# Softmax sums in an attention loop: adding the two key tiles of some pairs on GpSimd first

## The chip, the cores and the metric

The kernel runs on one core of a Trainium2 chip. TensorE (PE) does the matrix products, VectorE (DVE), ScalarE (ACT) and GpSimd (POOL) the elementwise work; SyncE (SP) and GpSimd issue the DMAs. The metric is the device time of one execution in microseconds (us).

## What is computed

Two layers of a mixer trunk over 2048 latent tokens and 256 context tokens, width 1024, in float32. The part that the change touches is the softmax attention of eight heads:

```
s = jnp.einsum('bqhd,bkhd->bhqk', qi, k).astype(jnp.float32) * sm_scale
p = jax.nn.softmax(s, axis=-1).astype(v.dtype)
return jnp.einsum('bhqk,bkhd->bqhd', p, v)
```

In both layers the 2048 latent queries attend to 2304 keys (latent and context). In the first layer alone the 256 context queries attend to the 256 context keys as well. Around it stand projections, a short and a long depthwise convolution, gates and an output projection.

## The kernel before

A layer runs four phases: token work, features with convolutions, attention, projection. The Python code unrolls everything; a planner that knows priorities (the order of the code, shifted where the code asks for it) and modelled durations then fixes the order of the instructions on each engine when the program is built. Each engine works through its own list in order.

Attention works in jobs of one head and 512 queries: 32 jobs a layer. A job goes through its 18 key tiles of 128 keys in nine pairs; in the first layer every fourth job has a tenth pair, for the context queries, half as wide. For a pair:

- TensorE makes the scores of either tile in three products (L1073 to L1075), as every float32 factor is split into a high and a low part.
- ScalarE takes the exponential twice, once at full precision into `p` (L1076) and once rounded into `ph` (L1077), for either tile.
- GpSimd subtracts: the residue `pl = p - ph`, both tiles in one instruction of 128x1024 (L1078).
- VectorE adds `p` of either tile into `acc`, a PSUM tile, for the softmax sum (L1085; the first tile of a job is copied, L1083): two instructions of 128x512.
- TensorE multiplies the values by `ph` (L1100) and `pl` (L1101) into `po`. These four products are put off in the code until the next pair's scores and residue are issued (`flush`).

`p` has four buffers, `ph` and `pl` three, the scores three PSUM banks, `acc` and `po` one each. At a job's end (`close`) ScalarE copies `acc` and `po` out, and TensorE and VectorE reduce the sums.

The softmax is shifted by the maximum of each query. The maxima are made ahead: for the next job, 20 products (L985) into two PSUM banks, each reduced by VectorE (L986, L989), then turned by TensorE (L994) and written by ScalarE as row 96 of `Q` (L995), so that the score product subtracts them. `ahead` spreads these steps over the pairs, three pairs early, at raised priority. A job's first score needs its turned maxima.

In the first layer a job also carries one column block of modulation weights: a split by ScalarE and GpSimd (L190, L191) and 16 short products (L216). GpSimd's queue issues the loads of the next head's K, Q and values (L961 to L967), four in four jobs.

Of the kernel before, what the change touches and what calls it, by code (L numbers as in the profile page):

```python
# [9 lines left out]
F32 = mybir.dt.float32  # L10
# [3 lines left out]
ALU = mybir.AluOpType  # L14
# [4 lines left out]
P = 128  # L19
# [65 lines left out]
def trunk(ctx: ExitStack, tc: tile.TileContext, ins, out):  # L85
    nc = tc.nc
    V, S, G, PE = nc.vector, nc.scalar, nc.gpsimd, nc.tensor

    def pool(stack, name, **kw):
        return stack.enter_context(tc.tile_pool(name=name, bufs=kw.pop("bufs", 1), **kw))  # L90
# [5 lines left out]
    def psum(tag, name):  # L96
        return ps.tile([P, 512], F32, tag=tag, name=name, bufs={"a": 3, "b": 2}.get(tag, 1))
# [841 lines left out]
    def attention(l, start):  # L939
        es = ExitStack()  # L940
        tp = pool(es, f"A{l}", reuse_waits="tile")
        vp = pool(es, f"Av{l}", reuse_waits="tile")
        op = pool(es, f"Ao{l}", reuse_waits="tile", side="right")
        hp = [pool(es, f"Aa{l}", reuse_waits="tile", side="right"), pool(es, f"Ab{l}", reuse_waits="tile")]
        mp = pool(es, f"Am{l}", reuse_waits="tile") if l < DEPTH - 1 else None
        last = l == DEPTH - 1
# [12 lines left out]
        def load(h):  # L959
            K = hp[h % 2].tile([97, NTT, 2, P], F32R, tag="K", name="K")  # L960
            G.dma_start(K[0:NOPE], kn_d[l][h])  # L961
            G.dma_start(K[NOPE:97], kr_d[l][h])
            Q = hp[h % 2].tile([97, NTT, 2, P], F32R, tag="Q", name="Q")
            nq_ = (SEQ if last else NT) // P
            G.dma_start(Q[0:QK, :nq_], q_d[l][h, :, :nq_])
            Vt = vp.tile([P, NTT, P], F32R, tag=f"V{h % 2}", name="Vt")
            G.dma_start(Vt, v_d[l][h])  # L967
            kv[h] = (K, Vt, Q)
# [39 lines left out]
        def ahead(idx, share):  # L1008

            while len(sums) <= idx + 1 and len(sums) <= len(jobs):  # L1010
                steps, ends = [], []
                for j in jobs[len(sums) - 1]:
                    a, finish, turn = prepare(*j)
                    steps += [[st] for st in a]
                    steps[-1].append(finish)
                    ends.append(turn)
                steps[-1] += ends
                queue.extend(steps)
                sums.append(sums[-1] + len(steps))
            if idx < len(jobs):  # L1020
                goal = sums[idx] + round(share * (sums[idx + 1] - sums[idx]))
                while sums[-1] - len(queue) < goal:
                    with tc.high_priority(offset=PO):
                        for st in queue.pop(0):
                            st()
# [7 lines left out]
        def split_mods():  # L1033
            for _ in range(min(len(mods), 2 if idx < MD else 1)):
                i, j = mods.pop(0)
                w = mp.tile([P, KD, P], F32, tag="wm", name="wm", bufs=2)
                hi, lo = (mp.tile([P, KD, P], F32R, tag="wm" + c, name="wm" + c, bufs=2) for c in "hl")
                ready.append((i, j, halves(i, j, [w], hi, lo, V if MV else None)))

        def use_mods():  # L1040
            while ready:
                i, j, parts = ready.pop(0)
                modulation(i, (j,), lambda _: parts, mp.tile([4, P], F32, tag="mrow", name="mrow", bufs=2))
# [4 lines left out]
        def flush():  # L1048
            for st in late:
                st()  # L1050
            late.clear()

        for idx, job in enumerate(jobs):
            h = job[0][0]
            if job[0][1] == (1024 if h else 512) and h + 1 < H:
                load(h + 1)
            pairs = [(j, it) for j in job for it in range(j[3], NTT, 2)]
            for pi, ((h, s, n, k0), kt0) in enumerate(pairs):
                if idx == len(jobs) - 1 and pi == len(pairs) - AE:
                    mark = tc.cur_priority  # L1060
                K, Vt, Q = kv[h]
                first, final = kt0 == k0, kt0 == NTT - 2
                if first:
                    po = psum("c", "po")
                    acc = psum("d", "acc")
                p = tp.tile([P, 2, 512], F32, tag="p", name="p", bufs=4)
                ph = tp.tile([P, 2, 512], F32R, tag="ph", name="ph", bufs=3)
                pl = tp.tile([P, 2, 512], F32R, tag="pl", name="pl", bufs=3)
                scs = []
                for z in range(2):  # L1070
                    kt, qt = kt0 + z, slice(s // P, (s + n) // P)
                    sc = psum("a", "sc")
                    PE.matmul(sc[:, :n], lhsT=K[0:97, kt, 0], rhs=Q[0:97, qt, 0], start=True, stop=False)  # L1073
                    PE.matmul(sc[:, :n], lhsT=K[0:QK, kt, 0], rhs=Q[0:QK, qt, 1], start=False, stop=False)  # L1074
                    PE.matmul(sc[:, :n], lhsT=K[0:QK, kt, 1], rhs=Q[0:QK, qt, 0], start=False, stop=True)  # L1075
                    S.activation(p[:, z, :n], sc[:, :n], AF.Exp, scale=scale)  # L1076
                    S.activation(ph[:, z, :n], sc[:, :n], AF.Exp, scale=scale)  # L1077
                G.tensor_tensor(pl[:, :, :n], p[:, :, :n], ph[:, :, :n].bitcast(F32), op=ALU.subtract)  # L1078
                flush()

                for z in range(2):
                    if first and z == 0:
                        V.tensor_copy(acc[:, :n], p[:, 0, :n])  # L1083
                    else:
                        V.tensor_tensor(acc[:, :n], acc[:, :n], p[:, z, :n], op=ALU.add)  # L1085
                for z in range(2):
                    at = pi + (z + 1) / 2 + LEAD
                    if at <= len(pairs):
                        ahead(idx + 1, at / len(pairs))
                    else:  # L1090
                        ahead(idx + 1, 1)
                        ahead(idx + 2, (at - len(pairs)) / len(pairs))
                if pi == len(pairs) // 2:
                    split_mods()
                if pi == len(pairs) - ME:
                    use_mods()

                def products(kt0=kt0, n=n, Vt=Vt, ph=ph, pl=pl, po=po, first=first, final=final):
                    for z in range(2):
                        PE.matmul(po[:, :n], lhsT=Vt[:, kt0 + z, :], rhs=ph[:, z, :n], start=first and z == 0, stop=False)  # L1100
                        PE.matmul(po[:, :n], lhsT=Vt[:, kt0 + z, :], rhs=pl[:, z, :n], start=False, stop=final and z == 1)  # L1101

                def close(h=h, s=s, n=n, po=po, acc=acc):
                    accs = op.tile([P, 512], F32, tag="o", name="accs", bufs=3)
                    S.activation(accs[:, :n], acc[:, :n], AF.Copy, scale=2.0)
                    o = op.tile([P, 512], F32, tag="o", name="o", bufs=3)
                    S.copy(o[:, :n], po[:, :n])
                    nc.sync.dma_start(o_d[l][h, :, s : s + n], o[:, :n])

                    nq = n // P  # L1110
                    px = psum("e", "psum_t")
                    for t in range(nq):
                        PE.transpose(out=px[:, t * P : (t + 1) * P], in_=accs[:, t * P : (t + 1) * P], identity=idn)
                    sm = tp.tile([P, 4], F32, tag="sm", name="sm", bufs=2)
                    V.tensor_reduce(sm[:, :nq], px[:, :n].rearrange("p (t k) -> p t k", k=P), axis=AX.X, op=ALU.add)
                    V.reciprocal(rinv[l][:, s // P : s // P + nq, h], sm[:, :nq])

                late.append(products)
                if final:
                    late.append(close)  # L1120
# [130 lines left out]
    for l in range(DEPTH):  # L1251
        for phase in (tokens, features, attention, project):
            if SEQP and f"{l}{phase.__name__[0]}" not in SEQP:
                continue
            mark = phase(l, since(mark))
# [54 lines left out]
```

## Time and profile before

| what | value |
|---|---|
| median of 3 runs | 3695.61 us (3680.32 to 3699.47) |
| the profiled execution's own time | 3695.0 us |
| its span, first to last instruction | 3693.2 us |
| mean granted TensorE clock, share of full speed | 0.978 |
| busy: TensorE, VectorE, ScalarE, GpSimd | 3529.8, 2888.8, 2166.7, 2341.6 us |
| attention, first layer: first and last start of L1078's instructions in it, about | 815 to 1740 us |
| attention, second layer: the same | 2611 to 3502 us |

Busy time is the time in which an engine has an instruction running. Matmuls are pipelined, so that a busy TensorE is not TensorE at its peak. A wait is put down to the instruction that ended last before it.

### The profile page before, as it was taken

What the parts mean: (1) busy time and instruction counts of PE and PEld (TensorE: products, weight loads), DVE (VectorE), ACT (ScalarE), POOL (GpSimd) and SP (SyncE); (2) the same over time, 40 slices, a digit from 0 to 9 for tenths busy, and PEclk for the clock granted to TensorE, in tenths of its full rate; (3) what the DMA queues carried; (4) which work ended last, traced back from release to release, by engine and by line L of the source; (5) the groups of instructions that cost most, each with busy time, mean ns of one, the idle gap of its engine ahead of it and who ended that gap; (6) DMA issues with size and microseconds to landing.
All of it is one profiled execution on the core that took longest, in us unless ns stands there. A gap on an engine that the chain in (4) does not pass through costs nothing. (4 is left out here: it accounts for less than half of the span.)

```text
span 3693.2 us, 52810 instructions
## 1 busy us (share of the span) xinstructions
PE 3529.8 (96%) x17532; PEld 2916.9 (79%) x17532; DVE 2888.8 (78%) x5472; ACT 2166.7 (59%) x4328; POOL 2341.6 (63%) x1497
## 2 busy tenths in 40 slices
PE   7899999999999999999999989999999999998999
PEld 5787888887888787877788878887777777776777
DVE  5986977877888888888437878769988888888832
ACT  4665343247778777877445663433677777776720
POOL 4664344348888888877435654444687887877721
PEclk8999999999999999999999999999999999999999
DMA  7567333433333213312776773435232202222163
GB/s 219 171 186 205 82 107 110 113 112 78 79 79 88 61 45 82 85 58 64 232 231 207 215 213 100 114 99 125 80 76 61 41 27 61 59 61 75 43 197 114
DMA packets 394386, 411.47 MB, mean 111 GB/s; under 512 B 19168, under 2 KB 332128, under 8 KB 388960
## 3 DMA queue, kind: packets, MB, share of 16 engines
q1 hardware_dynamic: 387712, 333.87, 31.2%
q0 software_dynamic: 6400, 74.22, 8.9%
q8 instruction: 138, 2.26, 0.3%
q14 instruction: 136, 1.11, 0.1%
HBM read 266.72 MB, written 141.59 MB: 111 GB/s over the span
## 5 line engine op out<-in xcount | busy, mean ns | idle before, releaser
L1078 POOL TENSOR_TENSOR pl<-p,ph 128x1024 fp32r<-128x1024 f32 (+1 forms) x584 | 1387.2, 2397 | 276.2 <-ACT ph L1077 110.4
L986 DVE TENSOR_REDUCE mx<-pmax 128x1 fp32r<-128x512 f32 (+1 forms) x1296 | 795.1, 628 | 122.0 <-PE pmax L985 113.6
L1076 ACT ACTIVATE p<-sc 128x512 f32<-128x512 f32 x1168 | 713.4, 612 | 240.5 <-PE sc L1075 232.7
L1085 DVE TENSOR_TENSOR acc<-acc,p 128x512 f32<-128x512 f32 x1096 | 756.7, 690 | 55.9 <-ACT p L1076 29.5
L1077 ACT ACTIVATE ph<-sc 128x512 fp32r<-128x512 f32 x1168 | 703.8, 612 | 20.1 <-PE po L1100 16.2
L194 PE MATMUL pf<-hhf,wh 128*128 128x256 f32 (+1 forms) x1584 | 549.3, 348 | 18.2 <-ACT tg L867 8.4
L196 PE MATMUL pf<-hhf,wl 128*128 128x512 f32 (+1 forms) x1584 | 546.4, 347 | 4.5 <-POOL wl L191 3.7
L195 PE MATMUL pf<-hlf,wh 128*128 128x256 f32 (+1 forms) x1584 | 547.2, 346 | 0.0
L985 PE MATMUL pmax<-K,Q 96*128 96x512 f32 (+1 forms) x1296 | 465.0, 386 | 34.8 <-DVE mx L986 26.8
L1073 PE MATMUL sc<-Q,K 97*128 97x512 f32 x1168 | 476.5, 408 | 11.7 <-ACT ph L1077 9.3
L1101 PE MATMUL po<-pl,Vt 128*128 128x512 f32 x1168 | 467.9, 401 | 2.1 <-POOL pl L1078 1.8
L1074 PE MATMUL sc<-Q,K 96*128 96x512 f32 x1168 | 465.2, 398 | 0.0
L1100 PE MATMUL po<-ph,Vt 128*128 128x512 f32 x1168 | 461.9, 396 | 1.1 <-DMA Vt<-v_d 0.8
L1075 PE MATMUL sc<-Q,K 96*128 96x512 f32 x1168 | 462.4, 396 | 0.0
L191 POOL TENSOR_TENSOR wl<-wraw,wh 128x1024 fp32r<-128x1024 f32 x104 | 253.8, 2441 | 292.8 <-ACT wh L190 279.4
L747 DVE SCALAR_TENSOR_TENSOR cacc<-z,hv,cacc 128x384 f32<-128x384 f32 (+5 forms) x780 | 403.0, 561 | 14.3 <-ACT cacc L742 11.2
L194 PEld LDWEIGHTS pf<-hhf,wh 128*128 128x128 f32 x1584 | 303.7, 192 | 57.2 <-ACT wh L190 9.1
L196 PEld LDWEIGHTS pf<-hhf,wl 128*128 128x128 f32 x1584 | 303.0, 192 | 44.3 <-POOL wl L191 7.2
L985 PEld LDWEIGHTS pmax<-K,Q 96*128 96x128 f32 x1296 | 245.3, 190 | 116.9 <-DVE mx L986 58.6
L195 PEld LDWEIGHTS pf<-hlf,wh 128*128 128x128 f32 x1584 | 303.8, 192 | 36.1
L1073 PEld LDWEIGHTS sc<-Q,K 97*128 97x128 f32 x1168 | 222.2, 190 | 71.3 <-ACT ph L1077 20.0
L1075 PEld LDWEIGHTS sc<-Q,K 96*128 96x128 f32 x1168 | 224.5, 192 | 51.5
(257 smaller groups left out, 6189.0 us busy)
## 6 DMA issues: line engine op xcount, KB each, us to landing
wraw<-in_w_in SPq DMA_DIRECT2D x108, 512.0 KB
q_d<-sg SPq DMA_DIRECT2D x68, 384.0 KB
wm<-in_w_mod SPq DMA_DIRECT2D x46, 512.0 KB
v_d<-vs SPq DMA_DIRECT2D x36, 512.0 KB
kn_d<-sg SPq DMA_DIRECT2D x72, 256.0 KB
K<-kn_d POOLq DMA_DIRECT2D x16, 1152.0 KB, 8.5
Vt<-v_d POOLq DMA_DIRECT2D x16, 1152.0 KB, 14.8
o_d<-o SPq DMA_DIRECT2D x64, 256.0 KB
```

The costliest lines, as they stand in the source:

```text
L194: PE.matmul(out_, lhsT=ahi, rhs=bhi, start=first, stop=False)
L195: PE.matmul(out_, lhsT=ahi, rhs=blo, start=False, stop=False)
L196: PE.matmul(out_, lhsT=alo, rhs=bhi, start=False, stop=last)
L985: PE.matmul(pm[:, :w], lhsT=Q[0:QK, s // P + t, 0], rhs=K[0:QK, a // P : (a + w) // P, 0], start=True, stop=True)
L986: V.tensor_reduce(part[:, t, c : c + 1], pm[:, :w], axis=AX.X, op=ALU.max)
L1073: PE.matmul(sc[:, :n], lhsT=K[0:97, kt, 0], rhs=Q[0:97, qt, 0], start=True, stop=False)
L1075: PE.matmul(sc[:, :n], lhsT=K[0:QK, kt, 1], rhs=Q[0:QK, qt, 0], start=False, stop=True)
L1076: S.activation(p[:, z, :n], sc[:, :n], AF.Exp, scale=scale)
L1077: S.activation(ph[:, z, :n], sc[:, :n], AF.Exp, scale=scale)
L1078: G.tensor_tensor(pl[:, :, :n], p[:, :, :n], ph[:, :, :n].bitcast(F32), op=ALU.subtract)
L1085: V.tensor_tensor(acc[:, :n], acc[:, :n], p[:, z, :n], op=ALU.add)
L1101: PE.matmul(po[:, :n], lhsT=Vt[:, kt0 + z, :], rhs=pl[:, z, :n], start=False, stop=final and z == 1)
```

## The change

For some pairs GpSimd adds the two tiles of `p` into a new tile `both` (two buffers) right behind the residue, and VectorE adds `both` to `acc` in one instruction. These are pairs 1, 4 and 7 of nine in the last layer, and pairs 1 and 4 in the first. The other pairs stay as they were. The sums are the same but for the order of the additions.

```diff
                 G.tensor_tensor(pl[:, :, :n], p[:, :, :n], ph[:, :, :n].bitcast(F32), op=ALU.subtract)
+                paired = pi % 3 == 1 and (last or pi < 6)
+                if paired:
+                    both = tp.tile([P, 512], F32, tag="both", name="both", bufs=2)
+                    G.tensor_tensor(both[:, :n], p[:, 0, :n], p[:, 1, :n], op=ALU.add)
                 flush()
 
-                for z in range(2):
-                    if first and z == 0:
-                        V.tensor_copy(acc[:, :n], p[:, 0, :n])
+                for x in [both[:, :n]] if paired else [p[:, z, :n] for z in range(2)]:
+                    if first:
+                        V.tensor_copy(acc[:, :n], x)
+                        first = False
                     else:
-                        V.tensor_tensor(acc[:, :n], acc[:, :n], p[:, z, :n], op=ALU.add)
+                        V.tensor_tensor(acc[:, :n], acc[:, :n], x, op=ALU.add)
+                first = kt0 == k0
```

## Rows read from the trace of the kernel before

**Rows 1.** The page: busy us, share of the span and instructions by engine.
```profile
PE 3529.8 (96%) x17532; PEld 2916.9 (79%) x17532; DVE 2888.8 (78%) x5472; ACT 2166.7 (59%) x4328; POOL 2341.6 (63%) x1497
```

**Rows 2.** Groups by form, layer 1, 2720 to 3263: busy, mean ns | idle before.
```profile
L1078 POOL TENSOR_TENSOR pl<-p,ph 128x1024 fp32r<-128x1024 f32 x180 | 428.4, 2402 | 104.3 <-PE pmax L985 58.6 <-issue 21.1 <-ACT ph L1077 16.8
L1085 DVE TENSOR_TENSOR acc<-acc,p 128x512 f32<-128x512 f32 x341 | 236.3, 693 | 25.9 <-ACT p L1076 18.4
```

**Rows 3.** Groups by form, layer 0, 936 to 1500.
```profile
L191 POOL TENSOR_TENSOR wml<-wm,wmh 128x1024 fp32r<-128x1024 f32 x20 | 47.9, 2393 | 26.6 <-ACT wmh L190 26.6
...
L1078 POOL TENSOR_TENSOR pl<-p,ph 128x512 fp32r<-128x512 f32 x5 | 6.5, 1298 | 0.1
```

**Rows 4.** Windows of attention: stretch, length; busy of PE, PEld, DVE, ACT, POOL; clock.
```profile
936.00:1500.00 564.00, 563.01 (x2786) 453.84 (x2784) 494.42 (x918) 444.42 (x836) 492.49 (x227) 1.00 0.29 72
...
2615.00:2720.00 105.00, 98.06 (x430) 77.79 (x431) 97.28 (x155) 76.37 (x147) 83.94 (x41) 0.98 0.22 53
2720.00:3263.00 543.00, 536.83 (x2362) 426.58 (x2361) 475.92 (x821) 410.22 (x781) 438.70 (x201) 1.00 0.23 52
3263.00:3505.00 242.00, 226.91 (x960) 176.55 (x959) 210.65 (x333) 175.69 (x345) 183.32 (x81) 0.96 0.25 65
```

**Rows 5.** Waits, layer 1, 2720 to 3263: us in total, times, longest.
```profile
PEld pmax L985 <- DVE mx L986: 19.3, 53, 0.6
...
PE pmax L985 <- DVE mx L986: 4.0, 16, 0.4
...
PEld po L1101 <- POOL pl L1078: 0.6, 2, 0.3
```

**Rows 6.** Waits, layer 0, 936 to 1500.
```profile
POOL wml L191 <- ACT wmh L190: 26.6, 10, 3.4
...
PEld pmax L985 <- DVE mx L986: 1.4, 5, 0.4
```

**Rows 7.** Waits, the opening of layer 1's attention, 2615 to 2720.
```profile
PE pmax L985 <- DVE mx L986: 6.5, 6, 2.7
```

**Rows 8.** Timeline, layer 0, one job: start, us, instruction, [idle before].
```profile
1069.54 0.48 PE L994 MATMUL pmt<-idr,mx 128*97 128x128 f32 x4
...
1075.61 0.22 PE L216 MATMUL pm<-wmh,s 128*4 128x128 f32 x1
...
1076.51 0.22 PE L216 MATMUL pm<-wml,s 128*4 128x128 f32 x1
...
1079.89 0.69 DVE L1083 COPY acc<-p 128x512 f32<-128x512 f32 x1 [0.73 <-ACT p L1076]
```

**Rows 9.** Timeline of TensorE, layer 1, the end of a job.
```profile
2989.72 0.40 PE L1073 MATMUL sc<-Q,K 97*128 97x512 f32 x1
2989.95 0.40 PE L1074 MATMUL sc<-Q,K 96*128 96x512 f32 x1
...
2994.17 0.50 PE L985 MATMUL pmax<-K,Q 96*128 96x512 f32 x1 [0.40 <-DVE mx L986]
2994.51 0.40 PE L1101 MATMUL po<-pl,Vt 128*128 128x512 f32 x1
...
2995.44 0.48 PE L994 MATMUL pmt<-idr,mx 128*97 128x128 f32 x4
...
2996.73 0.42 PE L1073 MATMUL sc<-Q,K 97*128 97x512 f32 x1
```

**Rows 10.** Timeline of GpSimd, layer 1, the same job.
```profile
2972.15 14.19 POOL L1078 TENSOR_TENSOR pl<-p,ph 128x1024 fp32r<-128x1024 f32 x6 [4.83 <-PE pmax L985]
2986.56 2.40 POOL L1078 TENSOR_TENSOR pl<-p,ph 128x1024 fp32r<-128x1024 f32 x1 [0.21 <-ACT ph L1077]
2989.14 2.41 POOL L1078 TENSOR_TENSOR pl<-p,ph 128x1024 fp32r<-128x1024 f32 x1 [0.17 <-ACT ph L1077]
2991.84 2.38 POOL L1078 TENSOR_TENSOR pl<-p,ph 128x1024 fp32r<-128x1024 f32 x1 [0.28 <-PE po L1100]
2999.85 2.41 POOL L1078 TENSOR_TENSOR pl<-p,ph 128x1024 fp32r<-128x1024 f32 x1 [5.63 <-PE pmax L985]
```

## The prediction, made before the result was known

> **What bounds the kernel now.** I read the page's busy shares first, then the windows of the two attention stages, then the waits inside them, and last the timeline at the seam between two jobs.
>
> TensorE is busy 96% of the span, VectorE 78%, GpSimd 63% [rows 1]. These are averages over stages; the change lives in attention alone, so the windows count. I chose one steady stretch of 20 jobs in each layer (180 residues at nine a job in [rows 2]; one split of modulation weights a job, x20, in [rows 3]). Layer 0: 564 us, so 28.2 us a job, TensorE 563.0 (99.8%), VectorE 494.4 (88%), GpSimd 492.5 (87%). Layer 1: 543 us, 27.15 us a job, TensorE 536.8 (98.9%), VectorE 475.9 (88%), GpSimd 438.7 (81%); the granted clock is 1.00, full speed, in both [rows 4]. So three engines stand close together and TensorE leads. A change that only empties VectorE can give back no more than what TensorE loses to VectorE.
>
> The waits say where that is. In layer 1's stretch the maximum products (L985) wait for VectorE's reductions (L986), which free their two PSUM banks: 19.3 us ahead of weight loads in 53 places and 4.0 us ahead of matmuls in 16 [rows 5]. In layer 0's stretch the same wait is 1.4 us [rows 6]. In the opening of layer 1's attention it is 6.5 us ahead of matmuls [rows 7].
>
> The timeline shows why the layers differ. In layer 0 the next job's shifts are turned (L994, at 1069.54) ten microseconds before that job's first add (1079.89) [rows 8]: the look-ahead maxima are done early. In layer 1 they are turned at 2995.44 and the next job's first score follows at 2996.73, just behind a maximum product that stood 0.40 us for VectorE [rows 9]. The maxima have fallen back to the last moment, because layer 1 has the shorter job with the same VectorE work. At that seam GpSimd stands idle too, 5.63 us between the last residue of one job and the first of the next; before it the residues run nearly back to back [rows 10].
>
> The Trainium skill (Perfetto Trace Analysis, Identifying the Most-Contended Engine) says matmul busy time is a poor measure of headroom and weight-load busy share a better one. The trace agrees: weight loads fill 453.8 of 564 us (80.5%) in layer 0 and 426.6 of 543 (78.6%) in layer 1 [rows 4], so the slack is layer 1's.
>
> **The change, part by part.** Paired are pairs 1 and 4 of nine in layer 0 (64 in its 32 jobs) and pairs 1, 4, 7 in layer 1 (96): 160.
>
> *Removed from VectorE:* one 128x512 add into PSUM for each, 0.693 us [rows 2]; 160 x 0.693 = 111 us, 2.08 us a job in layer 1, 1.39 in layer 0. In layer 0 nothing waits for it, so it is worth between 0 and 32/20 x 1.4 = 2 us; I take 0. In layer 1 it takes VectorE from 23.8 to 21.7 us a job, below layer 0's 24.7, in a job that is only 1 us shorter; the maxima should then run ahead as they do there. What that is worth has three measures. (a) TensorE's own idle time in the stretch, 543 - 536.8 = 6.2 us: 32/20 x 6.2 = 10 us over the layer. (b) Layer 0's pace: its stretch holds 424 matmuls more. 320 are modulation products at (1076.51 - 1075.61)/15 = 0.06 us [rows 8], 19 us; 50 belong to five context pairs, half of the 0.23 us spacing of a full one [rows 9], 6 us; the other 54, short ones, I estimate at 5 us. Without them layer 0 would take 534 us for what costs layer 1 543: 9 us, or 14 over 32 jobs. (c) All waits on the reductions, 23.3 us: 37 us over 32 jobs. The ends are 10 and 37; weight-load waits partly hide under a running matmul, but a matmul that starts late also hides inside the busy count, so I take the middle, 23.5 us. In the opening I take half of the 6.5 us, 3.2. The close of the layer, 3263 to 3505, loses 15.1 us of TensorE [rows 4], but VectorE splits output weights there too; I take nothing for it.
>
> *Added to GpSimd:* one 128x512 add each. The residue in that shape takes 1.298 us [rows 3], so 2.6 us a job in layer 0 and 3.9 in layer 1, 208 us in all. The bounds: nothing where GpSimd would have been idle, the whole 208 us where it is full. Layer 0: 24.6 + 2.6 = 27.2 of 28.2 us. Layer 1: 21.9 + 3.9 = 25.8 of 27.15. Both fit; what covers them is the idle time at the seam and between residues, so I take 0 in the steady stretches. If that cover were gone, the next residue would be late, then the product that reads it (L1101), and TensorE stops, as it works in order. At the end of the last job nothing covers them: the adds of pairs 4 and 7 delay the last residues, 2.6 us.
>
> The Trainium skill (GPSIMD Engine Reference, Engine selection) says elementwise adds belong on VectorE, since GpSimd is about twice as slow with two inputs. The trace agrees, 1.298 against 0.693 us; by that rule the change trades 111 us for 208 and should lose wherever GpSimd is full, which is the last rival below.
>
> *Moved and waiting:* VectorE's add for a paired pair now waits for GpSimd, a residue (2.40 us [rows 2]) and an add behind the exponentials. Queued behind it on VectorE are reductions, and the maximum products wait for these. If the planner puts the add too early, each costs up to 1.3 us of VectorE, 3.9 us a job in layer 1, against the 2.08 us saved; but VectorE idles 12%, and the order is made with the dependency known: 0 taken, and the upper end is another way into the second case. ScalarE reuses a p buffer only after GpSimd's add, one of four buffers, so 0. The loads of a head's keys, queries and values sit in GpSimd's queue (four issues for four jobs); they move by an add or two and are issued about a job before their first use: 0. Matmul counts, DMAs and exponentials do not change.
>
> **Sum.** -23.5 - 3.2 + 2.6 = -24.1 us, on the profiled execution's own 3695.0 us: 3671 us. The median shown is 3695.6, so the reference is the same. 0.5% is 18.5 us, about what runs spread over 19 us can tell from no change.
>
> **The rivals.**
> *Forecast, 0.50:* layer 1's maxima catch up. 3671 us, own range 3655 to 3688. For it: the wait is almost wholly in layer 1, and VectorE loses exactly there the most. Against it: the planner's order, not only the durations, sets the seam.
>
> *Nothing measurable, 0.26:* 3688 us. TensorE's floor is closer than I think (measure (a), 10 us), and some of it is paid back in waits for residues. For it: TensorE is 98.9% busy already [rows 4].
>
> *GpSimd becomes the bound, 0.24:* slower, about 3718. Place: the last residues of a job. In layer 1 three adds push the ninth residue by 3 x 1.3 less the 0.66 us of gaps among the last residues, 3.2 us; it ended at 2991.84 + 2.38 = 2994.22 and its product started at 2994.51 [rows 9, 10], so 0.3 us is slack and up to 2.9 us a job, 93 us, could reach TensorE. In layer 0 GpSimd also stands 26.6 us in 20 jobs behind the modulation weights' ScalarE copy [rows 6] with 2.39 us residues of weights behind it [rows 3]: 27.2 + 1.3 = 28.5 against 28.2, 0.3 us a job, 10 us. It decides from the point where the seam's 5.63 us no longer takes up the lateness; I price it at 10 us in layer 0 and a seventh of the 93, 13, in layer 1, with the forecast's gain gone: 3695 + 23 = 3718. It reaches from 3705, layer 0 alone, to 3798, all of it. Against it: today TensorE waits 0.6 us for residues in 543 [rows 5], and the seam's idle time is larger than the adds.
>
> **How the numbers follow.** The forecast case lies beyond -0.5% in four of five of its outcomes: 0.40, and 0.10 within. The second case is within, save 0.02 faster and 0.01 slower. The third is slower in 0.20 and within in 0.04. Faster 0.42, same 0.37, slower 0.21. The range runs from 3652, which is measure (c) with the opening and layer 0's 2 us (3695 - 37 - 3 - 2 = 3653), to 3714, just short of the third case's middle; some 0.06 is left out below and 0.13 above.
>
> **What would show it.** Right: layer 1's jobs at about 26.4 us, the wait of maximum products for reductions down from 23.3 us in 20 jobs to under 8, the turn of the shifts several microseconds ahead of the next job's scores, GpSimd at 93 to 97% in both layers, and 160 adds of about 1.3 us. Wrong: weight loads or matmuls of L1101 waiting for residues by more than 10 us a stretch, layer 0's job longer than 28.3 us, or VectorE's adds waiting for GpSimd with reductions queued behind them. A longer stall at the change of stages, where VectorE's and ScalarE's orders are made anew, would make the time wrong without touching the argument.

## The result, and the profile after

The change made the kernel slower: 3731.6 us median (3727.5 to 3733.8, six runs) against 3693.1 us, ratio 1.0103, 95% interval 1.0084 to 1.0123. Forecast was 3671, with 3652 to 3714 as the range: the kernel got slower where it was to get faster, and the time lies outside. The profiled execution took 3733.8 us, its span is 3732.0 against 3693.2. In the changed kernel the lines behind L1078 have moved: GpSimd's add is L1082, VectorE's adds are L1090 (L1085 before), the products L1106 and L1107 (L1100, L1101), the copies that close a job L1111 and L1113.

The page's busy line and the windows of the 20 steady jobs in either layer (columns as in [rows 4]):

```profile
PE 3547.5 (95%) x17532; PEld 2910.1 (78%) x17532; DVE 2796.5 (75%) x5312; ACT 2207.2 (59%) x4328; POOL 2534.9 (68%) x1657
```
```profile
943.00:1524.00 581.00, 572.42 (x2779) 452.82 (x2778) 473.55 (x874) 454.43 (x836) 540.99 (x267) 1.00 0.28 70
...
2752.00:3298.00 546.00, 541.79 (x2381) 423.97 (x2380) 449.73 (x780) 427.63 (x781) 512.31 (x261) 1.00 0.22 52
```

Against [rows 1] VectorE lost 92 us and GpSimd gained 193. GpSimd is busy 93% (541.0 of 581) and 94% (512.3 of 546), where [rows 4] has 87% and 81%. Layer 0's 20 jobs now need about 580 us in place of 564. Groups by form in layer 1, 2752 to 3298:

```profile
L1078 POOL TENSOR_TENSOR pl<-p,ph 128x1024 fp32r<-128x1024 f32 x180 | 429.4, 2401 | 33.6 <-ACT ph L1077 23.0 <-DVE mx L986 6.3 <-DVE acc L1090 1.5
...
L1107 PE MATMUL po<-pl,Vt 128*128 128x512 f32 x362 | 143.7, 397 | 0.0
...
L1082 POOL TENSOR_TENSOR both<-p 128x512 f32<-128x512 f32 x60 | 77.4, 1290 | 0.0
```

The add takes 1.29 us, as estimated, and GpSimd's idle time ahead of residues fell from 104.3 [rows 2] to 33.6 us. TensorE never waits for a residue (0.0 ahead of L1107). The waits of the same stretch, and then those of layer 0, 943 to 1524:

```profile
PEld sc L1073 <- ACT ph L1077: 26.2, 80, 0.6
...
ACT ph L1077 <- PE po L1106: 8.1, 30, 0.6
...
PEld pmax L985 <- DVE mx L986: 4.5, 12, 1.0
...
PE sc L1073 <- ACT ph L1077: 1.8, 11, 0.2
...
PE pmax L985 <- DVE mx L986: 0.9, 3, 0.6
```
```profile
ACT ph L1077 <- PE po L1106: 30.5, 55, 3.8
...
PEld pmax L985 <- DVE mx L986: 14.8, 29, 3.8
PEld sc L1073 <- ACT ph L1077: 12.1, 34, 0.6
PE pmax L985 <- DVE mx L986: 6.0, 8, 3.4
```

In layer 1 the wait of maximum products for reductions did fall, from 19.3 + 4.0 [rows 5] to 4.5 + 0.9 us. In its place the score products wait 28 us for ScalarE: a score bank comes free when `ph` is written, and `ph` is written when a product has read the buffer it reuses. In layer 0 there is no gain to set against this: the wait for reductions rose from 1.4 us [rows 6] to 20.8.

Where the 39 us lie is read from the starts of the ScalarE copies of `po` that close the jobs. Two of them, at the ends of heads 0 and 6 in layer 1:

```profile
2762.26 0.59 ACT L1113 COPY o<-po 128x512 f32<-128x512 f32 x1
...
3415.18 0.65 ACT L1113 COPY o<-po 128x512 f32<-128x512 f32 x1
```

(3415.18 - 2762.26) / 24 jobs = 27.21 us a job. "First head", also called the opening, is the time from the layer's first score to the copy that ends head 0. The last column counts the matmuls that start in the stage.

| stage, us | before | after | difference | matmuls |
|---|---|---|---|---|
| layer 0, first head | 130.4 | 140.6 | +10.2 | 623, 643 |
| layer 0, 24 steady jobs | 28.20 each | 28.95 each | +18.0 | 3332, 3331 |
| layer 0, last head | 133.3 | 124.0 | -9.3 | 546, 519 |
| between the attentions | 845.9 | 841.0 | -4.9 | 4281, 4289 |
| layer 1, first head | 129.3 | 147.4 | +18.1 | 533, 567 |
| layer 1, 24 steady jobs | 27.06 each | 27.21 each | +3.6 | 2818, 2839 |
| layer 1, last head | 133.0 | 135.8 | +2.8 | 493, 458 |
| all else | | | +0.3 | 4906, 4886 |

The stages do not hold the same work: the new order makes products for later jobs earlier, in the openings, and the last heads have fewer left. At the 0.23 us spacing of [rows 9] an estimate for the same work is +6, +18 and -3 us in layer 0, and +10, -1 and +11 in layer 1 (first head, steady jobs, last head).

So three places carry the loss: layer 0's jobs, the openings and the last head of layer 1. In that last head TensorE is idle 19.3 us in place of 12.3, and its matmuls wait for ScalarE ahead of their scores (3.1 us before); the waits from 3415 to 3551:

```profile
PE sc L1073 <- ACT ph L1077: 12.1, 20, 2.2
```

The opening of layer 1 can be followed in the timeline. First GpSimd in the changed kernel, then VectorE, then TensorE:

```profile
2636.23 2.38 POOL L1078 TENSOR_TENSOR pl<-p,ph 128x1024 fp32r<-128x1024 f32 x1
2638.59 1.28 POOL L1082 TENSOR_TENSOR both<-p 128x512 f32<-128x512 f32 x1
2639.84 4.65 POOL L1078 TENSOR_TENSOR pl<-p,ph 128x1024 fp32r<-128x1024 f32 x2
...
2638.02 6.62 DVE L164 TENSOR_SCALAR csq<-cva 128x264 int32<-128x264 int32 x1
2644.56 0.68 DVE L986 TENSOR_REDUCE mx<-pmax 128x1 fp32r<-128x512 f32 x1
...
2645.30 1.33 PE L985 MATMUL pmax<-K,Q 96*128 96x512 f32 x2 [4.72 <-DVE mx L986]
...
2703.72 1.20 PE L985 MATMUL pmax<-K,Q 96*128 96x512 f32 x2 [4.46 <-DMA Q<-q_d]
```

L164 is a shift of integer words from SBUF to SBUF, part of a reciprocal root that the stage still owes. Its record lasts from 2638.02 to 2644.64, and GpSimd's unbroken row of four instructions ends at 2644.49. The reduction behind it on VectorE is late, TensorE stands 4.72 us for it, and 58 us on it stands another 4.46 us for a load of Q. The same row in the kernel before, with GpSimd beside it:

```profile
2621.99 2.53 DVE L164 TENSOR_SCALAR csq<-cva 128x264 int32<-128x264 int32 x1
...
2621.97 2.40 POOL L1078 TENSOR_TENSOR pl<-p,ph 128x1024 fp32r<-128x1024 f32 x1 [0.58 <-POOL pl L1078]
2624.85 2.40 POOL L1078 TENSOR_TENSOR pl<-p,ph 128x1024 fp32r<-128x1024 f32 x1 [0.48 <-ACT ph L1077]
```

There a gap of 0.48 us came after one residue, at 2624.37, and L164 ended at 2624.52. But the long hold adds little to the sum. Waits of the whole opening, after (2615 to 2762) and then before (2599 to 2728):

```profile
PE pmax L985 <- DVE mx L986: 8.5, 7, 4.7
...
PE pmax L985 <- DMA Q<-q_d: 4.5, 1, 4.5
```
```profile
PE pmax L985 <- DVE mx L986: 7.0, 8, 2.7
```

Before, more of VectorE's instructions were held, each for a shorter time. Nor did the load of Q, which is that of the next head, come late. The first is its issue after, the second the first product that reads it before:

```profile
2684.34 0.52 POOL L965 DMA_DIRECT2D Q<-q_d  x1
```
```profile
2694.00 0.63 PE L985 MATMUL pmax<-K,Q 96*128 96x512 f32 x2
```

The load was issued 69.5 us behind the layer's first score, 68.8 before (at 2667.67), and landed 19.2 us on, 19.1 before. Its first reader is the layer's 81st product of L985, as the first head's four jobs have 20 each. That reader was next in TensorE's order 84.4 us behind the first score, where before it came at 95.2. The order had drawn the look-ahead forward; the load stayed where it was.

The last part is TensorE's granted clock. The windows of the whole opening, after and then before (the clock is the third last figure), each with the stretches in it at 0.50, which is 1.2 GHz:

```profile
2615.00:2762.00 147.00, 132.47 (x567) 103.52 (x566) 118.36 (x195) 96.03 (x178) 114.98 (x65) 0.93 0.28 68
...
2642.50:2649.33 6.83, 4.03 (x9) 3.10 (x10) 6.76 (x12) 0.60 (x1) 1.98 (x1) 0.50 0.00 0
2659.57:2666.40 6.83, 5.97 (x14) 4.72 (x15) 5.53 (x11) 3.62 (x7) 2.37 (x1) 0.50 0.00 0
2700.53:2707.36 6.83, 3.64 (x11) 3.01 (x12) 1.56 (x3) 1.50 (x3) 0.78 (x2) 0.50 0.14 31
```
```profile
2599.00:2728.00 129.00, 120.77 (x533) 94.74 (x533) 115.10 (x187) 88.56 (x170) 95.40 (x50) 0.99 0.30 74
...
2643.68:2647.09 3.41, 3.41 (x10) 2.64 (x9) 3.41 (x7) 2.73 (x7) 1.78 (x1) 0.50 0.00 0
```

The first and the third of these begin within the stops of 4.72 and 4.46 us. TensorE is busy 13.6 us at the lower clock in place of 3.4; half of that is lost against full speed, an estimated 6.8 us in place of 1.7. In all TensorE stands idle 14.5 us in place of 8.2 and is busy 11.7 us longer. By estimate 5 of the 11.7 us are the clock, and the rest, about 7, goes to the 34 matmuls more (8 us at 0.23). Of the 6.3 us more of idle time 4.5 are the wait for Q and 1.5 the reductions.

### The profile page after: what moved, and what is told of

The parts are those of the page before. It is cut to its first block, busy times and chain, and to the rows that moved or that the text cites. A ratio compares the mean times of both kernels' runs of the same rounds, so it can differ in the third digit from the quotient of the medians.

```text
span 3732.0 us, 52967 instructions
## 1 busy us (share of the span) xinstructions
PE 3547.5 (95%) x17532; PEld 2910.1 (78%) x17532; DVE 2796.5 (75%) x5312; ACT 2207.2 (59%) x4328; POOL 2534.9 (68%) x1657
## 5 line engine op out<-in xcount | busy, mean ns | idle before, releaser
L1078 POOL TENSOR_TENSOR pl<-p,ph 128x1024 fp32r<-128x1024 f32 (+1 forms) x584 | 1386.4, 2390 | 157.2 <-ACT ph L1077 105.8
L1076 ACT ACTIVATE p<-sc 128x512 f32<-128x512 f32 x1168 | 692.9, 599 | 298.8 <-PE sc L1075 277.3
L1077 ACT ACTIVATE ph<-sc 128x512 fp32r<-128x512 f32 x1168 | 644.4, 596 | 92.6 <-PE po L1106 83.9
L194 PE MATMUL pf<-hhf,wh 128*128 128x256 f32 (+1 forms) x1584 | 549.4, 348 | 19.1 <-ACT tg L867 8.3
L1090 DVE TENSOR_TENSOR acc<-acc,p 128x512 f32<-128x512 f32 (+1 forms) x776 | 535.8, 691 | 29.0 <-ACT p L1076 2.4
L1073 PE MATMUL sc<-Q,K 97*128 97x512 f32 x1168 | 490.6, 420 | 21.6 <-ACT ph L1077 19.1
L985 PE MATMUL pmax<-K,Q 96*128 96x512 f32 (+1 forms) x1296 | 448.4, 387 | 44.7 <-DVE mx L986 33.7
L1107 PE MATMUL po<-pl,Vt 128*128 128x512 f32 x1168 | 467.3, 400 | 0.0
L1106 PE MATMUL po<-ph,Vt 128*128 128x512 f32 x1168 | 463.1, 397 | 0.7 <-DMA Vt<-v_d 0.7
L985 PEld LDWEIGHTS pmax<-K,Q 96*128 96x128 f32 x1296 | 245.7, 191 | 119.2 <-DVE mx L986 58.1
```

Source lines behind the costliest of these rows:

```text
L194: PE.matmul(out_, lhsT=ahi, rhs=bhi, start=first, stop=False)
L985: PE.matmul(pm[:, :w], lhsT=Q[0:QK, s // P + t, 0], rhs=K[0:QK, a // P : (a + w) // P, 0], start=True, stop=True)
```

## The experiments

Each ratio is to the runs of the kernel before beside it, with its 95% interval; "layer 1: first head, steady job" are the stages of the table above. The table has all of them; the diffs below are against the changed kernel unless said.

| run | us | ratio | layer 0: first head, steady job | layer 1: first head, steady job |
|---|---|---|---|---|
| the change | 3731.6 | 1.0103 (1.0084-1.0123) | 140.6, 28.95 | 147.4, 27.21 |
| layer 1 alone | 3722.6 | 1.0073 (1.0054-1.0092) | 130.4, 28.19 | 147.2, 27.21 |
| layer 0 alone | 3700.6 | 1.0010 (0.9997-1.0022) | 140.6, 28.98 | 130.0, 27.00 |
| relief only | 3691.6 | 0.9989 (0.9976-1.0003) | 132.1, 28.29 | 127.7, 26.96 |
| load only | 3725.9 | 1.0074 (1.0056-1.0092) | 140.1, 28.74 | 150.3, 27.28 |
| products first | 3729.0 | 1.0089 (1.0068-1.0111) | 142.8, 28.65 | 148.1, 27.21 |
| four `ph`, `pl` | 3724.0 | 1.0077 (1.0055-1.0099) | 144.7, 28.56 | 143.8, 27.12 |
| narrow add | 3676.9 | 0.9960 (0.9942-0.9979) | 134.2, 28.76 | 130.9, 26.64 |
| add later | 3731.9 | 1.0096 (1.0074-1.0118) | 140.7, 28.99 | 147.0, 27.21 |
| planned with a fast GpSimd | 3835.8 | 1.0375 (1.0354-1.0396) | 134.9, 29.38 | 138.0, 30.72 |
| its control | 3737.6 | 1.0106 (1.0089-1.0124) | 130.4, 28.87 | 128.1, 28.07 |
| one pair, layer 1 | 3689.9 | 0.9979 (0.9967-0.9991) | 131.3, 28.18 | 127.9, 27.05 |
| two pairs, layer 1 | 3694.1 | 1.0001 (0.9989-1.0013) | 130.7, 28.21 | 142.6, 26.48 |
| two, not first head | 3688.7 | 0.9979 (0.9965-0.9992) | 131.4, 28.19 | 129.2, 26.75 |
| change, not first heads | 3699.4 | 1.0003 (0.9990-1.0017) | 130.1, 28.81 | 129.1, 27.25 |
| one pair, layer 0 | 3678.9 | 0.9944 (0.9925-0.9963) | 138.0, 27.96 | 129.1, 27.07 |
| two pairs and weights moved, layer 0 | 3719.5 | 1.0061 (1.0041-1.0080) | 143.3, 29.12 | 130.5, 27.00 |
| weights moved alone | 3724.7 | 1.0080 (1.0055-1.0105) | 134.3, 28.95 | 129.0, 27.07 |
| one pair, then two, not first heads | 3674.8 | 0.9941 (0.9919-0.9964) | 130.3, 28.10 | 129.1, 26.77 |

The jobs of a layer that a run leaves alone repeat within 0.1 us, but its last head and the stages behind do not: layer 1's last head is 127.0 us where layer 0 alone was changed, 133.0 before, with 493 matmuls in both. Differences of under about 10 us in a total are therefore not read as effects of an edit.

**Either layer alone.**

```diff
-paired = pi % 3 == 1 and (last or pi < 6)
+paired = last and pi % 3 == 1
```

> Pairs 1, 4, 7 of the last layer alone; the first layer as before. The trace of the changed kernel puts some 20 us of its 38 into the first layer's attention and some 20 into the last layer's (opening and close above all). If the loss is a cost of the loaded stretch itself, this kernel loses the last layer's half: 3710 to 3716. If the loss of the last layer came from what the first layer did to the order, about 3693.

```diff
+paired = not last and pi % 3 == 1 and pi < 6
```

> Pairs 1 and 4 of the first layer alone. Cost of the loaded stretch: first layer's jobs at 29.0 us as in the changed kernel, 3710 to 3716 in all, and the last layer's jobs back at 27.15 us.

The two layers are independent: each layer's attention is as in the full change (147.2 and 27.21; 140.6 and 28.98). Layer 1 alone costs 0.7%; layer 0 alone costs 19 us inside its attention, but the total shows 0.1%, as the stages behind it came out shorter.

**Relief and load apart.** One run keeps VectorE's saving without GpSimd's add, and leaves the second tile out of the sum; the other keeps GpSimd's add without the saving.

```diff
-both = tp.tile(...)
-G.tensor_tensor(both[:, :n], p[:, 0, :n], p[:, 1, :n], op=ALU.add)
+both = p[:, 0]
...
-V.tensor_copy(acc[:, :n], x)
+V.tensor_scalar(acc[:, :n], x, 1e-3, None, op0=ALU.add)
```

> The same 160 pairs, but GpSimd's add is left out and VectorE adds the first tile alone (the second tile's share of the sum is missing, and a constant of 0.001 is added at a job's start in its place). VectorE's relief without its price. If VectorE's reductions hold the last layer back as priced in the prediction: 3665 to 3675, the last layer's jobs at 26.4 us. If TensorE's floor is closer: 3683 to 3693. Any time above 3700 would say that the new order alone costs, without GpSimd.

```diff
-for x in [both[:, :n]] if paired else [p[:, z, :n] for z in range(2)]:
+for x in [p[:, z, :n] for z in range(2)]:
```

> GpSimd makes its 160 adds, but VectorE adds both tiles itself as before, so that nothing reads GpSimd's sum: the price without the relief and without VectorE's new wait. If GpSimd's load is the cause: 3731 or more, up to 3770. If VectorE's wait for GpSimd is the cause: about 3693.

The load alone costs 0.74%, the greater part of the loss of 1.03%. The relief alone is worth nothing that can be told from no change. Its waits in layer 1, 2752 to 3295, and its window there:

```profile
PEld pmax L985 <- DVE mx L986: 19.7, 52, 0.6
...
PE pmax L985 <- DVE mx L986: 5.5, 21, 0.4
```
```profile
2752.00:3295.00 543.00, 536.09 (x2367) 425.67 (x2368) 439.13 (x763) 410.16 (x780) 438.61 (x201) 1.00 0.23 52
```

VectorE went from 475.9 to 439.1 us of 543 and the wait for its reductions stayed, 25 us against 23.3 [rows 5]. With the load only, VectorE is as full as before (484.1 us), and the wait falls to 10.9:

```profile
PEld pmax L985 <- DVE mx L986: 8.6, 22, 1.0
...
PE pmax L985 <- DVE mx L986: 2.3, 5, 0.7
```

So that wait is not made by VectorE's load.

**Is it the wait of VectorE for the add, or the add's place?** The narrow add keeps the instruction and its dependency but works on 64 of 512 columns (the rest of the second tile is left out of the sum); the other run puts the add behind the next pair's residue.

```diff
-both = tp.tile(...)
-G.tensor_tensor(both[:, :n], p[:, 0, :n], p[:, 1, :n], op=ALU.add)
+both = p[:, 0]
+G.tensor_tensor(both[:, :64], p[:, 0, :64], p[:, 1, :64], op=ALU.add)
...
-V.tensor_copy(acc[:, :n], x)
+V.tensor_scalar(acc[:, :n], x, 1e-3, None, op0=ALU.add)
```

> GpSimd adds only the first 64 of 512 columns (the rest of the second tile is missing from the sum; 0.001 is added at a job's start), and VectorE's add still waits for it. The wait and the instructions stay, GpSimd's time goes down to about 0.3 us an add. If GpSimd's time costs, planned or real: 3690 to 3705. If the new wait of VectorE on GpSimd costs: 3715 to 3731.

```diff
+for q, bt in owed:      # behind this pair's residue
+    G.tensor_tensor(bt[:, :n], q[:, 0, :n], q[:, 1, :n], op=ALU.add)
+    V.tensor_tensor(acc[:, :n], acc[:, :n], bt[:, :n], op=ALU.add)
+owed.clear()
...
-both = ...; G.tensor_tensor(both[:, :n], ...)
+owed.append((p, tp.tile([P, 512], F32, tag="both", name="both", bufs=2)))
...
-for x in [both[:, :n]] if paired else [p[:, z, :n] for z in range(2)]:
+for x in [] if paired else [p[:, z, :n] for z in range(2)]:
```

> GpSimd's add put behind the residue of the next pair, and VectorE's add behind that: same work, the next residue no longer waits for the add. If the loss is the delay of the next residue: 3695 to 3710. If it is GpSimd's total load (planned or real): 3720 to 3735.

Neither. With a GpSimd instruction of 0.32 us in each place the kernel is faster than before (0.996), and the add in another place changes nothing (1.0096). So in layer 1 the length of GpSimd's add counts, and not its presence. Whether it counts on the chip or by the order that the planner makes for it, no run separates. The narrow add's window there:

```profile
2752.00:3295.00 543.00, 538.41 (x2407) 432.90 (x2407) 447.45 (x775) 414.33 (x798) 464.16 (x265) 1.00 0.22 53
```

GpSimd at 85%, and TensorE gets through 2407 matmuls in 543 us where the relief alone gets through 2367: the 26.64 us a job are near the 26.4 that were forecast.

**Products late, or too few buffers?** From a residue's end to the start of the product that reads it, paired from the records of layer 1, the median is 4.1 us after the change and 1.8 before. One run raises the priority of the products, one gives `ph` and `pl` a fourth buffer.

```diff
-for st in late:
-    st()
+with tc.high_priority(offset=40):
+    for st in late:
+        st()
```

> The changed kernel with the value products given a higher priority (40 places earlier) in the planner. In the changed kernel they start 3.8 to 4.1 us after their residue has ended (median), before 1.8 to 2.1. If priority alone puts them behind the scores: the lag falls to 2 us or less and the time to 3690 to 3705. If the planner holds them back because it thinks GpSimd later than it is: lag and time as in the changed kernel, 3725 to 3735. If GpSimd on the chip is the bound: the products come earlier and TensorE waits for residues, 3725 or more.

```diff
-ph = tp.tile([P, 2, 512], F32R, tag="ph", name="ph", bufs=3)
-pl = tp.tile([P, 2, 512], F32R, tag="pl", name="pl", bufs=3)
+ph = tp.tile([P, 2, 512], F32R, tag="ph", name="ph", bufs=4)
+pl = tp.tile([P, 2, 512], F32R, tag="pl", name="pl", bufs=4)
```

> The changed kernel with four buffers in place of three for ph and for pl. If TensorE stalls since late products hold the three ph buffers, so that ScalarE can't write and the scores find no bank: 3690 to 3705, and the wait of scores for ph gone. If GpSimd's rate is the bound, buffers don't help: 3725 to 3735.

The first changed nothing in layer 1, the second gave back 8 us of 38, less than the 10 us above. With four buffers the weight loads of the scores still wait 21.0 us for ScalarE in layer 1 (26.2 in the change). The buffer is where the wait shows; that it makes it is not shown.

**Does the planner take GpSimd for slower than it is?**

```diff
+TRN2Spec.GPSIMD_TENSOR_TENSOR_READ_CYCLES = tuple(c * 0.5 for c in TRN2Spec.GPSIMD_TENSOR_TENSOR_READ_CYCLES)
```

> The changed kernel's instructions, but the planner is told that GpSimd reads its two inputs in half the cycles, so that it plans a residue and an add some tenth shorter than they are; the chip's own durations can't change. If the loss comes from the order (products planned behind a GpSimd that looks full): products follow their residues sooner than 3.8 us, and the time falls to 3690 to 3710. If GpSimd on the chip is the bound: TensorE now waits for residues, 3725 or more.

The control is the kernel before, planned in the same way.

> The kernel before with the same setting of the planner, as a control. Its products stand 1.8 to 2.1 us behind their residues; 3685 to 3705 either way, and more if the planner's shorter times make TensorE run into residues that aren't ready.

This theory got no support. Ordered for a GpSimd that reads its two inputs in half the cycles, the kernel loses 3.75%, and its control 1.06%, so the setting costs by itself. Waits in layer 1 of the first, 2780 to 3330 (its lines are one further on):

```profile
PEld po L1108 <- POOL pl L1079: 32.7, 57, 1.9
```

Here TensorE does wait for residues: the median product starts 0.6 us behind its residue, in the change 4.1. That argues that the late products of the change's order spare it that wait.

**How many pairs in layer 1.**

```diff
+paired = last and pi == 4          # one pair
+paired = last and pi in (1, 4)     # two pairs
```

> One pair in nine (pair 4), last layer alone. GpSimd has 21.9 + 1.3 = 23.2 us of work in a job of 27.15. Order or fullness should not bite here: 3680 to 3697, jobs 26.6 to 27.2 us. If any added GpSimd time costs in proportion, a third of the last layer's 25 us: 3704.

> Two pairs in nine (1 and 4), last layer alone: 24.5 of 27.15 us. Loss in proportion: 3713. A threshold near fullness: as before, 3685 to 3700.

None, one, two and three pairs give 27.06, 27.05, 26.48 and 27.21 us a steady job. The window of two pairs, 2752 to 3295:

```profile
2752.00:3295.00 543.00, 540.12 (x2417) 433.04 (x2416) 458.61 (x794) 431.76 (x801) 499.56 (x247) 1.00 0.23 53
```

GpSimd stands at 92% and the gain is there; with a third pair, at 94%, it is gone, also if the 21 matmuls more that these 24 jobs then hold are taken off (an estimated 0.2 us a job). But two pairs also bring the long first head, 142.6 us, which eats it.

**The openings.**

```diff
+paired = last and idx >= 4 and pi in (1, 4)                      # two, not first head
+paired = pi % 3 == 1 and (last or pi < 6) and idx >= 4           # the change, not first heads
```

> Pairs 1 and 4 of each job of layer 1, but none in its first head (56 adds on GpSimd). With two pairs everywhere in layer 1 the steady jobs fell to 26.48 us and the first head rose from 129 to 143 us, and the total stood at 1.000. Theory 'full where it is added' (the adds of the first head themselves cost the opening): first head 128 to 131 us, steady jobs 26.5, total 3678 to 3684, ratio 0.996. Rival 'order of the stage' (the planner makes another opening as soon as later jobs hold two adds, or the opening's length is chance of the order): first head 140 us or more, total 3692, ratio 1.000.

> The changed kernel without its adds in the first head of each layer (140 adds). 'Full where it is added': layer 1's first head back at 129 us (from 147) and layer 0's at 130 (from 141), the steady jobs as in the changed kernel (28.95 and 27.21), total 3731 - 18 - 10 = 3703, ratio 1.003. 'Order of the stage': both openings stay, total 3725 to 3731.

Without the adds of the first heads (20 of 160), both openings are back at 130.1 and 129.1 us and the total falls from 3731.6 to 3699.4: the adds of the first heads themselves cost the openings, with the later ones in place. Both openings then hold as many matmuls as before (623 and 533). The 24 jobs of layer 1 hold 52 more (2870); for the same work their 27.25 us would be an estimated 26.75, so in this kernel the third pair does not undo all of the gain. L164 takes 2.53 us again:

```profile
2614.51 2.53 DVE L164 TENSOR_SCALAR csq<-cva 128x264 int32<-128x264 int32 x1
```

Over the runs the length of L164 in layer 1's opening goes with the first head: 0.30 us and 127.9 (one pair), 2.53 and 129 (before; two runs without the first head), 4.11 and 142.6 (two pairs), 6.62 and 147 (the change), 7.50 and 150.3 (load only); the narrow add has 1.74 and 130.9. The wait for the load of Q, 4.0 to 5.2 us (1.6 with four buffers), stands in all of these from 4.11 us up and in none below; so do more matmuls in the first head (554 to 567, against 531 to 545) and more time at the lower clock (13.7 to 20.5 us against 3.4 to 6.8). So these come together. That L164 is the start of them is not shown: all VectorE instructions that were held in the opening lost about 13 us in sum before and 12 in the change, as estimated from the shortest record of each.

**Layer 0: GpSimd too full, or the order?** Three runs: one pair; two pairs with the modulation weights' residue moved from GpSimd to VectorE; and that move alone in the kernel before.

```diff
+paired = not last and pi == 4                 # one pair
...
-MV = 0
+MV = 1                                        # with two pairs in layer 0; and alone
```

> One paired pair (pair 4) in each job of layer 0, none in layer 1 (32 adds). GpSimd's work in a steady job of layer 0 is 24.6 + 1.3 = 25.9 of 28.2 us, 92%. 'Full' (it bites from about 94%): steady jobs 28.2 to 28.3, total 3690 to 3697. Rival 'order' (any add on GpSimd ahead of VectorE's makes the planner's order worse in layer 0; the narrow add of 0.32 us had 28.76 us a job there): steady jobs 28.5 to 28.8, total 3700 or more.

> Two pairs in each job of layer 0 as in the change, none in layer 1, and the residue of the modulation weights (2.40 us a job on GpSimd) made by VectorE. GpSimd is at 24.6 + 2.6 - 2.4 = 24.8 of 28.2 us, as full as before; VectorE gains about 1 us a job on balance. 'Full': steady jobs back to 28.2 to 28.3 us (28.98 with the two adds alone), total 3690 to 3697. 'Order': steady jobs stay at 28.7 to 29.0, total 3700 or more.

> Control for the run with two pairs in layer 0: the kernel before, with the residue of the modulation weights made by VectorE in layer 0 and nothing else changed. GpSimd's work falls to 22.2 of 28.2 us a job. If moving that residue does no harm by itself, steady jobs of layer 0 stay at 28.2 us or fall a little and the total is 3690 to 3697: then the 29.12 us of the run with two adds speaks for 'order', since GpSimd was at 85% there. If the jobs go to 29 us here too, the move itself costs them, and the run with two adds says nothing on either theory.

The windows of layer 0, 943 to 1510, of the first, the second and the third:

```profile
943.00:1510.00 567.00, 565.90 (x2809) 456.79 (x2809) 486.06 (x906) 455.43 (x849) 521.82 (x249) 1.00 0.30 73
```
```profile
943.00:1510.00 567.00, 555.83 (x2681) 439.62 (x2680) 487.58 (x871) 436.46 (x806) 479.20 (x234) 0.99 0.28 69
```
```profile
943.00:1510.00 567.00, 560.37 (x2702) 442.35 (x2701) 506.77 (x913) 432.31 (x816) 435.27 (x199) 1.00 0.28 69
```

One pair, with GpSimd at 92%, is faster than before: 27.96 us a job, ratio 0.9944, which was not expected. GpSimd at 85% with two pairs and at 77% with none are slow, 29.12 and 28.95; the move itself costs what the two adds cost, so the second run can't settle the question. The third shows, with the narrow add (28.76 us, GpSimd at 88%), that a full GpSimd is not needed for a slow job here.

**A version from the runs.**

```diff
+paired = idx >= 4 and (pi == 4 or last and pi == 1)
```

> A version put together from the runs: no add on GpSimd in the first head of either layer, one pair (4) in each later job of layer 0, two (1 and 4) in each later job of layer 1. From the stages: layer 0's steady jobs 27.96 us against 28.20 (24 x 0.24 = 5.8 us) and its last head 4 us less, layer 1's 26.5 to 26.75 us against 27.06 (24 x 0.3 to 0.55 = 7 to 13 us) and its last head 3 us less: 3695 - 20 to 26 = 3669 to 3675, ratio 0.993 to 0.995. If the gains of one pair in layer 0 were chance of the order, 3688, ratio 0.998, as with layer 1's pairs alone.

3674.8 us, ratio 0.9941 (0.9919 to 0.9964): faster than both kernels, by 20 us and by 57. From 2752 to 3298 in layer 1 GpSimd is at 91% (499.26 of 546) and TensorE gets through 2421 matmuls, 2381 in the change.

## Why the prediction was wrong

*The step that failed* is "Both fit; what covers them is the idle time at the seam and between residues, so I take 0 in the steady stretches". GpSimd's load alone (load only) costs 0.74%, and layer 0's jobs, priced at 0, took 0.75 us more each, 18 us in all. Its bounds were named, "nothing where GpSimd would have been idle, the whole 208 us where it is full", and GpSimd's share afterwards, 93 to 97%, was forecast well; the error was to let idle time in a sum stand for cover.

*Layer 1's steady jobs*, -23.5 us: measured +3.6. The forecast sign, the wait for reductions down to under 8 us, came (23.3 to 5.4 us), and with two pairs or the narrow add so did most of the gain (26.48 and 26.64 us a job against 26.4). But the cause was not the one given. VectorE's relief alone left the wait at 25 us. With GpSimd's load and no relief it fell to 10.9 us. So the -23.5 stood on a wait that VectorE's load does not make; the runs argue that the planned order of products and reductions makes it, and no run separates that further. In the change, with the third add, the score products wait 28 us for ScalarE, and the gain is gone.

*The opening of layer 1*, -3.2 us: measured +18.1, by estimate +10 for the same work. Half of its 6.5 us wait for reductions was to go; over the whole opening that wait rose from 7.0 to 8.5 us. The forecast had no term for look-ahead products that are drawn forward, nor for the clock. And "they move by an add or two and are issued about a job before their first use: 0" failed in its second half: the load of Q moved 0.7 us, but its first reader was next 15 us behind the issue in place of 26, and TensorE stood 4.46 us for it.

*Layer 0*, 0: measured +18 in the steady jobs and +10 in the first head. The forecast named "layer 0's job longer than 28.3 us" as a sign of being wrong, and it came, 28.95. TensorE waits there for reductions (20.8 us against 1.4) and for ScalarE ahead of its scores (12.1 us against 3.5). The second in the kernel before, 936 to 1500:

```profile
PEld sc L1073 <- ACT ph L1077: 3.5, 15, 0.3
```

That GpSimd's adds bring this is shown (load only, 28.74); that it is because GpSimd is full is not, since one pair at 92% gains and three kernels between 77 and 88% have slow jobs. Why this layer's order turns at the second add stays open.

*VectorE's wait for the adds*, 0: right as far as is shown. It is 15.9 us in five places of the whole trace, all in the last heads, and the narrow add, which keeps that dependency, gains.

*The close*, +2.6 us: layer 1's last head measured +2.8, which is luck. It holds 35 matmuls fewer, so that the same work cost an estimated 11 us more, in a stage that scatters by 6, and what TensorE waits for there is ScalarE ahead of the scores, which the forecast did not have.

*The rivals.* "GpSimd becomes the bound", given 0.24, had the right sign; its 3718 was 14 us short and its range to 3798 held the time. Its place, the last residues and the products that read them, was wrong: TensorE waited 0.0 us for residues, as the products start 4.1 us behind their residues (median of layer 1); in layer 1 part of the loss shows up one step on, at the score banks. The rule of the Trainium skill that stood beside it (GPSIMD Engine Reference, Engine selection), by which 111 us of VectorE are traded for 208 of GpSimd, pointed the right way; the runs agree for the full change (1.0103) and not for one add in layer 0's jobs (0.9944).

## What to carry to other kernels

Idle time in an engine's sum is no cover until one sees what stands behind each gap: GpSimd had 13 to 19% idle in the steady stretches, and adds that fit into it still cost 0.7% without the relief. Give away such work one instruction at a time and leave the opening of a stage alone; about half of these adds (84 of 160) gained 0.6%, all of them lost 1.0%. Where a planner makes the order, part the relief from the load in two runs before the wait is put down to a busy engine, and count the matmuls of a stage before its time is compared.

## What was not expected of the hardware

Two VectorE instructions from SBUF to SBUF were held until GpSimd's row of instructions had a gap, not only until the current one ended. L164 lasted 6.62 us over parts of four GpSimd instructions, none longer than 2.41; in the run with one pair, where it fell into a gap of GpSimd, it took 0.30. Again in layer 0, first VectorE, then GpSimd, then TensorE:

```profile
1235.47 5.48 DVE L232 SCALAR_TENSOR_TENSOR gain<-mod,vec 128x16 f32<-128x16 f32 x1
...
1232.63 7.07 POOL L1078 TENSOR_TENSOR pl<-p,ph 128x1024 fp32r<-128x1024 f32 x3
1239.65 1.26 POOL L1082 TENSOR_TENSOR both<-p 128x512 f32<-128x512 f32 x1
...
1241.61 0.50 PE L985 MATMUL pmax<-K,Q 96*128 96x512 f32 x1 [3.41 <-DVE mx L986]
```

L232 ends at 1240.95, 0.04 us behind GpSimd's row, and takes 0.16 us elsewhere; here it cost TensorE 3.41 us. VectorE's reductions and adds that read PSUM keep their 0.69 us beside the same GpSimd work. Not every instruction waits for a gap. In the kernel before, VectorE's L800, also from SBUF to SBUF, was let in behind the one GpSimd instruction in its way, though the next followed without a gap; first VectorE, then GpSimd:

```profile
2652.64 2.96 DVE L800 SCALAR_TENSOR_TENSOR cc<-csq,cc 128x264 f32<-128x264 f32 x2
...
2650.22 5.09 POOL L1078 TENSOR_TENSOR pl<-p,ph 128x1024 fp32r<-128x1024 f32 x2 [2.53 <-PE po L1101]
2655.27 1.64 POOL L191 TENSOR_TENSOR zl<-cc,zh 128x264 fp32r<-128x264 f32 x2
```

The second L800 ends at 2655.60, 0.29 us behind the residue's end. What makes the difference stays open. The Trainium skill (SBUF — State Buffer, Who interferes with whom) says that the two engines share a port pair, which for some kinds of VectorE instruction one of them holds while the other is fully blocked until the holder's instruction is finished. The trace agrees with the block; for L800 its length is that of one instruction, for L164 and L232, 6.62 and 5.48 us, it is that of the whole row.
